# A new order for the mixer of a macaron layer, interleaved score products, and a second norm whose squares are summed by a matrix of ones

## The chip, the cores and the metric

One core of one Trainium2 chip runs the whole layer as a single program. The metric is the device time of one execution in microseconds (us): the median of several runs. A change of this kernel by less than about 0.2% (1.6 us) can't be told from no change.

## The reference

One encoder layer on x of 512 tokens by 1024 channels, in float32: half a SwiGLU feed-forward, a mixer, another half feed-forward, and a last norm. The mixer is the part that the change touches:

```python
def rmsnorm(x, g):
    y = x * lax.rsqrt(jnp.mean(x * x, axis=-1, keepdims=True) + EPS)
    return y * g

def hybrid_mixer(h, w_in, q_gain, k_gain, rel_bias, pool_w, pool_scale, w_out):
    proj = h @ w_in                       # 1024 -> q, k, v, u of 512 columns each
    ...
    a = chunked_attention(q, k, v, q_gain, k_gain, rel_bias)   # 8 heads of 64, q and k normed per head
    p = multiscale_pool(u, pool_w, pool_scale)                 # 4 groups, windows 2, 4, 8, 16
    return jnp.concatenate([a, p], axis=-1) @ w_out

x = x + 0.5 * swiglu_ffn(rmsnorm(x, ffn1_norm), ...)
x = x + hybrid_mixer(rmsnorm(x, mix_norm), ...)
x = x + 0.5 * swiglu_ffn(rmsnorm(x, ffn2_norm), ...)
x = rmsnorm(x, final_norm)
```

Attention is causal by chunks of 64 frames (own chunk and 8 before), with a bias that depends on the distance alone.

## The kernel before, in words

**Products.** Everything is kept transposed, with channels on the partitions and the 512 tokens along the free axis, in eight tiles x[0] to x[7]. A float32 product is made as three products of rounded parts (`mm3`, L270 to L276): high by high (L274), low by high (L275), high by low (L276). A split into high and low parts is a cast or scale on ACT (L157, L160) and a subtraction on DVE (L158, L161), and weights of the mixer are split by L1235 on ACT and L1237 on DVE. `mm3` streams its moving operand "woven" (L252): column 0, column 256, column 1, column 257 and so on, and whoever reads the result takes it apart again with `back` (L255), a strided read of PSUM.

**Stages.** The first feed-forward runs to about 321 us of the trace, the mixer to about 475 us, the second feed-forward and the last norm to the end. There are eight PSUM banks, four for `mm` tiles and four for `a` tiles.

**The mixer** is a set of coroutines that the program runs while it is built: `products` (the projections in the order of `ORDER`: q and k of heads 0 to 3, q and k of heads 4 to 7, u, v, u, u, u, then the output projection), `finish_norm`, `qk_norm`, `scores` for each pair of heads, `softmax` for each head and tile of 128 queries, `head` (transposes of the probabilities, L1506, and the product with v, L1518), `pool` and `pool_map`. Each yields when it would have to wait, by a model of four clocks (`on`, `until`), and the first one in order of rank that can run goes on (`run_parts`, L1160). The result is a fixed order of instructions for each of PE, ACT, DVE and GpSimd. So the numbers `RANK_...`, `RANKS`, `SLACK`, `POOL_AFTER`, `NORM`, `NORM_AT` and `FILL_AT` at the head of the file set the order and nothing else; the hardware then waits on semaphores.

**The second norm.** The squares of x are added up into `acc`, a 128x512 tile (L385). `per_token` (L387) multiplies `acc` by a column of ones, four 128x1 products in full float32 (L389), which gives the sum of squares of each token on its partition. ACT takes a rough inverse root of it (L396) and DVE makes one Newton step (L360 to L362); the result is `r`, 128x4, by which q, k and v are scaled when they leave PSUM (L1315, L160/L161). For u, where tokens lie along the free axis, the same numbers are needed along rows: DVE writes two diagonal matrices with the high and low parts of `r` (L401 to L405), PE multiplies them by ones (L414), and ACT copies the bank to `rb` (L422), which L1567 uses.

**q and k.** The four token tiles of a q and k projection leave their banks by L1315 on ACT (times `r`), are squared by L1331 on ACT, summed per head by L1334 on DVE, go through the integer-started root L337 to L349 on DVE, are scaled by L1365 on DVE, and are transposed by L1374 on PE.

**Scores.** For a pair of heads, the two lie in rows 0 to 63 and 64 to 127 of the same tiles, so L1454 issues two products at a time, one in each half of the array, into two banks. `GROUPS` lists for each pair which query tiles share a bank: pair 0 has ((2, 0),) and then ((3,), (1,)), pairs 1 and 3 have (1, 0), (2,), (3,), and pair 2 the reverse. `softmax`: bias and row maximum on DVE (L1416), exponent on ACT (L1423), reciprocal on DVE (L1426), scaling on ACT (L1429).

**v and u.** Each 128x512 tile of v leaves its bank in two halves, each by L160 on ACT and then L161 on DVE. u leaves by L1567 on DVE, and GpSimd makes the trailing sums (L1577).

## Time and profile before

| what | value |
|---|---|
| runs | 807.75, 807.83, 808.76 us; median 807.83 |
| the profiled execution's own time | 808.83 us |
| its span, first to last instruction | 807.0 us (1.83 us lie outside it) |
| mean granted TensorE clock | 0.999 |
| DVE, ACT, GpSimd busy | 88%, 62%, 12% of the span |
| instructions | 14153 |

In a line of the timeline the first two numbers are start and duration in us, then come the engine, the line of the kernel, the operation, the output and the input, and how many such instructions in a row were taken together; in brackets stands how long the engine was idle before it, and on whom it waited. PE's matmuls overlap: a 128x512 product is shown with 0.38 us, but one starts every 0.216 us, so PE's time is read from one start to the next.

### The profile page before, as it was taken

What the parts mean: (1) busy time and instruction counts of PE and PEld (TensorE: products, weight loads), DVE (VectorE), ACT (ScalarE), POOL (GpSimd) and SP (SyncE); (2) the same over time, 40 slices, a digit from 0 to 9 for tenths busy, and PEclk for the clock granted to TensorE, in tenths of its full rate; (3) what the DMA queues carried; (4) which work ended last, traced back from release to release, by engine and by line L of the source; (5) the groups of instructions that cost most, each with busy time, mean ns of one, the idle gap of its engine ahead of it and who ended that gap; (6) DMA issues with size and microseconds to landing.
All of it is one profiled execution on the core that took longest, in us unless ns stands there. A gap on an engine that the chain in (4) does not pass through costs nothing.

```text
span 807.0 us, 14153 instructions
## 1 busy us (share of the span) xinstructions
PE 797.8 (99%) x5273; PEld 735.5 (91%) x5273; DVE 710.3 (88%) x1163; ACT 503.8 (62%) x873; POOL 100.1 (12%) x148
## 2 busy tenths in 40 slices
PE   9999999999999999999999999999999999999996
PEld 8889999999988888888878888899999999988886
DVE  7999999899897878876979778999989999896997
ACT  8456555666676657558657756565566655766574
POOL 0111111222011100101111000201121111010100
PEclk9999999999999999999999999999999999999999
DMA  8677778988799973332212137858878888799942
GB/s 311 184 210 203 185 214 247 208 201 216 200 270 314 310 241 105 118 118 92 78 54 79 53 132 250 268 160 224 216 213 230 213 199 210 222 305 339 320 144 104
DMA packets 79414, 160.61 MB, mean 199 GB/s; under 512 B 7393, under 2 KB 30705, under 8 KB 78961
## 3 DMA queue, kind: packets, MB, share of 16 engines
q1 hardware_dynamic: 56256, 113.16, 41.7%
q0 software_dynamic: 22656, 46.14, 27.2%
q8 instruction: 41, 0.67, 0.3%
q10 hardware_dynamic: 432, 0.41, 0.1%
q14 instruction: 29, 0.23, 0.1%
HBM read 153.38 MB, written 50.34 MB: 252 GB/s over the span
## 4 chain that ended last, share of the span: by engine, by line
PE 86%; DVE 7%; ACT 4%; issue 2%; DMA 1%; SPq 0%; DVEq 0%; ACTq 0%
PE mm L274 20%; PE mm L275 20%; PE mm L276 20%; PE a L276 7%; PE a L275 7%; PE a L274 7%; DVE wlo L158 1%; PE a L1518 1%; PE a L1506 1%; ACT prob L1423 1%; ACT prob L1429 1%; ACT whi L1235 1%; PE a L1454 1%; DVE prob L1416 1%; DVE wlo L1237 1%
## 5 line engine op out<-in xcount | busy, mean ns | idle before, releaser
L158 DVE TENSOR_TENSOR wlo<-raw,whi 128x1024 fp32r<-128x1024 f32 (+1 forms) x110 | 120.6, 1107 | 17.7 <-ACT whi L157 17.6
L157 ACT CAST whi<-raw 128x1024 fp32r<-128x1024 f32 (+1 forms) x110 | 103.2, 951 | 38.1 <-PE mm L276 14.8
L939 POOL DMA_DIRECT2D wsum<-in_wB_dram x72 | 70.2, 1086 | 447.8 <-DVE t L843 222.1
L275 PE MATMUL mm<-ha,whi 128*128 128x256 f32 x420 | 115.5, 275 | 0.0
L276 PE MATMUL mm<-ha,wlo 128*128 128x256 f32 x420 | 115.5, 275 | 0.0
L274 PE MATMUL mm<-ha,whi 128*128 128x256 f32 x420 | 115.5, 275 | 0.0
L788 ACT ACTIVATE t<-mm 128x256 f32<-128x256 f32 x105 | 40.4, 385 | 113.6 <-PE mm L276 113.1
L600 DVE TENSOR_TENSOR wlo<-wsum,whi 128x1024 fp32r<-128x1024 f32 x70 | 85.5, 1221 | 9.8 <-ACT whi L595 9.8
L274 PEld LDWEIGHTS mm<-ha,whi 128*128 128x128 f32 x420 | 80.6, 192 | 0.1
L275 PEld LDWEIGHTS mm<-ha,whi 128*128 128x128 f32 x420 | 80.6, 192 | 0.1
L276 PEld LDWEIGHTS mm<-ha,wlo 128*128 128x128 f32 x420 | 80.6, 192 | 0.0
L595 ACT CAST whi<-wsum 128x1024 fp32r<-128x1024 f32 x70 | 70.0, 1047 | 3.7 <-DVE wsum L619 2.0
L275 PE MATMUL mm<-wlo,ah 128*128 128x512 f32 x176 | 67.0, 380 | 0.1
L276 PE MATMUL mm<-whi,ah 128*128 128x512 f32 x176 | 66.7, 379 | 0.0
L274 PE MATMUL mm<-whi,ah 128*128 128x512 f32 x176 | 66.5, 379 | 0.0
L274 PE MATMUL mm<-hhi,whi 128*128 128x512 f32 x168 | 64.5, 384 | 0.0
L600 DVE TENSOR_TENSOR wlo<-raw,whi 128x512 fp32r<-128x512 f32 x70 | 64.1, 955 | 0.0
L275 PE MATMUL mm<-hlo,whi 128*128 128x512 f32 x168 | 63.7, 379 | 0.0
L276 PE MATMUL mm<-hhi,wlo 128*128 128x512 f32 x168 | 63.7, 379 | 0.0
L595 ACT CAST whi<-raw 128x512 fp32r<-128x512 f32 x70 | 57.9, 828 | 1.9 <-PE mm L275 1.9
L158 DVE TENSOR_TENSOR ah<-acts,ah 128x512 fp32r<-128x512 f32 (+1 forms) x72 | 45.7, 646 | 10.9 <-ACT ah L157 10.8
L157 ACT CAST ah<-acts 128x512 fp32r<-128x512 f32 (+1 forms) x72 | 40.6, 581 | 20.4 <-PE mm L275 13.8
(246 smaller groups left out, 2331.6 us busy)
## 6 DMA issues: line engine op xcount, KB each, us to landing
raw<-in_wA_dram SPq DMA_DIRECT2D x142, 256.0 KB, 3.9
wsum<-in_wB_dram POOLq DMA_DIRECT2D x60, 512.0 KB, 7.2
raw<-wsum SPq DMA_DIRECT2D x40, 512.0 KB, 6.3
raw<-in_wB_dram SPq DMA_DIRECT2D x30, 512.0 KB, 8.4
wsum<-wsum POOLq DMA_DIRECT2D x20, 512.0 KB, 5.7
raw<-in_wA_dram SPq DMA_DIRECT2D x16, 512.0 KB, 4.6
x<-in_xT_dram SPq DMA_DIRECT2D x16, 256.0 KB, 6.4
raw<-in_wQK_dram SPq DMA_DIRECT2D x8, 512.0 KB, 3.4
```

Source lines behind the costliest of these rows:

```text
L157: last_cast[0] = nc.scalar.copy(hi, src)
L158: nc.vector.tensor_tensor(lo, src, hi.bitcast(F32), op=ALU.subtract)
L274: nc.tensor.matmul(acc, a[0], b[0], start=start, stop=False, **more)
L275: nc.tensor.matmul(acc, a[0], b[1], start=False, stop=False, **more)
L276: return nc.tensor.matmul(acc, a[1], b[0], start=False, stop=stop, **more)
L595: nc.scalar.copy(hi, src)
L600: nc.vector.tensor_tensor(lo, src, hi.bitcast(F32), op=ALU.subtract)
L788: nc.scalar.activation(two(dst), back(src), AF.Copy, scale=scale)
L939: begun = nc.gpsimd.dma_start(self.rows(i, g), self.rows(self.terms[i][at], g), **(dict(accum_op=ALU.add) if at else {}),)
L1235: nc.scalar.copy(hi, raws[i])
L1237: nc.vector.tensor_tensor(lo, raws[i], hi.bitcast(F32), op=ALU.subtract)
L1416: nc.vector.tensor_tensor_reduce(p, sc, bias[h][0][:, S - n :], -1.0, BIG, op0=ALU.add, op1=ALU.min, accum_out=nm)
```

## The change

**The second norm.** `finish_norm` no longer calls `per_token` and `spread`. It splits `acc` into high and low parts (ACT, DVE) and sends them through two 128x512 products with a matrix of ones (`over_rows`, the call that the third norm uses in `steps`, L425). Every row of the bank then holds the sum of squares of all 512 tokens. From it DVE picks each token's own sum with the identity (four 128x128 multiply-and-add reductions), ACT and DVE make `r` as before, and ACT (one 128x512 root) and DVE (128x512 `v`, then three more 128x512 operations in the new part `spread`) make `rb` without PE.

**The scores.** The moving operand is now woven, so softmax reads the bank through `back`. With `SHARED = 1, 2`, the second head of pairs 1 and 2 is to take the upper half of the first head's bank wherever a group is `(1,)` alone.

**The order.** The ranks and the numbers for the clocks are replaced, `NORM_AT` goes from 3 to 2, `FILL_AT` from 7 to 6, `AHEAD_AT` from 8 to 7.

```diff
-RANK_QK, RANK_HEAD, RANK_POOL, RANK_SCORES = 1.66, 1.47, 0.935, 0.92
+RANK_QK, RANK_HEAD, RANK_POOL, RANK_SCORES = 1.82, 1.42, 1.335, 0.82
-POOL_AFTER = (8, 8, 7, 6)
+POOL_AFTER = (7, 3, 5, 7)
+SHARED = 1, 2
-            nc.vector.tensor_tensor_reduce(
-                p, sc, bias[h][0][:, S - n :], -1.0, BIG, op0=ALU.add, op1=ALU.min, accum_out=nm
+            nc.vector.tensor_tensor_reduce(
+                two(p), back(sc), two(bias[h][0][:, S - n :]), -1.0, BIG, op0=ALU.add, op1=ALU.min,
+                accum_out=nm,
             )
...
-                for _ in group:
+                for ts in group:
                     sc.append([])
-                    for h in heads:
-                        sc[-1].append((yield from take("a")))
+                    for i in range(2):
+                        if i and ts == (1,) and pair in SHARED:
+                            sc[-1].append((sc[-1][0][0][:, S // 2 :], sc[-1][0][1]))
+                        else:
+                            acc = yield from take("a")
+                            sc[-1].append((acc, ["a"] * len(ts) * (2 if ts == (1,) and pair in SHARED else 1)))
...
-                                    kT[pair][0][b][rows, :n], start=a + b == 0, stop=a == 1,
+                                    woven(kT[pair][0][b][rows, :n]), start=a + b == 0, stop=a == 1,
...
         def finish_norm():
             while used[0] < NORM_AT:
                 yield None
+            pair = temp(F32R), temp(F32R)
+            split(n2.acc, *pair)
+            f = on("dve", t_dve(S), on("act", t_act(S)))
+            yield from until(f + NORM)
             total = yield from take("a")
-            n2.per_token(total)
-            f = on("dve", NORM, on("pe", 0.45))
+            n2.over_rows(total, pair)
+            f = on("pe", 0.45)
+            yield from until(f, "act", "dve")
+            total = back(total)
+            wide, junk = temp(), temp()
...
+            for t in range(NT):
+                z = slice(t % 2 * P, (t % 2 + 1) * P)
+                nc.vector.tensor_tensor_reduce(
+                    junk[:, :P], total[:, t // 2, z], ident, 1.0, 0.0, op0=ALU.mult, op1=ALU.add,
+                    accum_out=ss[:, t : t + 1],
+                )
+                f = on("dve", t_dve(P))
+            nc.scalar.activation(root, ss, AF.Abs_reciprocal_sqrt, scale=1.0 / D, bias=eps)
+            nc.vector.tensor_scalar(v, ss, 1.0 / D, EPS, op0=ALU.mult, op1=ALU.add)
+            rsqrt_of(v, root, n2.r)
+            on("dve", 0.8, on("act", 0.3))
+            nc.scalar.activation(
+                two(wide), total, AF.Abs_reciprocal_sqrt, scale=1.0 / D, bias=eps
+            )
+            nc.vector.tensor_scalar(two(junk), total, 1.0 / D, EPS, op0=ALU.mult, op1=ALU.add)
+            f = on("dve", t_dve(S), on("act", t_act(S)))
             room["a"].append(f)
-            yield from until(f)
-            wide = yield from take("a")
-            n2.spread(wide)
-            room["a"].append(on("act", t_act(S), on("pe", 0.9)))
+            start(spread(wide, junk, f), 8)
+
+        def spread(y, v, f):
+            yield from until(f, "dve")
+            sq = temp()
+            nc.vector.tensor_tensor(sq, y, y, op=ALU.mult)
+            nc.vector.scalar_tensor_tensor(v, sq, -0.5, v, op0=ALU.mult, op1=ALU.mult)
+            n2.rb = n2.broadcast()
+            nc.vector.scalar_tensor_tensor(n2.rb, v, 1.5, y, op0=ALU.add, op1=ALU.mult)
+            on("dve", 3 * t_dve(S))
```

How the instructions stand, at three places. The numbers behind the names tell tiles apart; the line numbers after the change are 22 to 28 higher (L274 is L296, L414 is L436, L161 is L183, L1429 is L1453).

PE in the q and k projection of heads 4 to 7, before: the four 128x1 products of the norm stand between the products of the sixth weight tile with token tiles 0 and 1 (`mm_4128` and `mm_4132` are the banks of those token tiles).

```order
L275 MATMUL mm_4128<-wlo_4122,hhi_4040 128x512
L276 MATMUL mm_4128<-whi_4121,hlo_4041 128x512
L389 MATMUL a_4215<-ones,acc_3897 128x1 x4
L274 MATMUL mm_4132<-whi_4121,hhi_4040 128x512
L275 MATMUL mm_4132<-wlo_4122,hhi_4040 128x512
```

and seven products of `mm3` further on, still before, the pair with ones that makes `rb`:

```order
L274 MATMUL mm_4140<-whi_4121,hhi_4053 128x512
L275 MATMUL mm_4140<-wlo_4122,hhi_4053 128x512
L276 MATMUL mm_4140<-whi_4121,hlo_4054 128x512
L414 MATMUL a_4259<-t_4234,ones_r 128x512
L414 MATMUL a_4259<-t_4235,ones_r 128x512
L274 MATMUL mm_4128<-whi_4176,hhi_4066 128x512
L275 MATMUL mm_4128<-wlo_4177,hhi_4066 128x512
```

The same stretch of PE's row after, where the pair with ones makes the sums themselves:

```order
L296 MATMUL mm_4128<-whi_4121,hhi_4053 128x512
L297 MATMUL mm_4128<-wlo_4122,hhi_4053 128x512
L298 MATMUL mm_4128<-whi_4121,hlo_4054 128x512
L436 MATMUL a_4231<-t_4185,ones_r 128x512
L436 MATMUL a_4231<-t_4186,ones_r 128x512
L296 MATMUL mm_4132<-whi_4121,hhi_4053 128x512
L297 MATMUL mm_4132<-wlo_4122,hhi_4053 128x512
L298 MATMUL mm_4132<-whi_4121,hlo_4054 128x512
```

L389 has no counterpart, and the pair with ones stands three `mm3` (nine products) earlier among its neighbours; the number of products with ones is the same.

DVE while v leaves its banks (`mm_4728`, `mm_4732`, `mm_4742`, `mm_4775` before are the banks of the four tiles of v; `bias` is the widened bias of a head, `m` a half of a pooled group or of a transposed q or k, `wlo` a weight's low part), before:

```order
L1237 TENSOR_TENSOR wlo_4980<-raw_4852,whi_4979 128x1024
L161 SCALAR_TENSOR_TENSOR v_4996<-mm_4728,r_4222,v_4996 128x4x64 x2
L1426 RECIPROCAL rt_4963<-tot_4962 128x1
L1274 STREAM_SHUFFLE bias_5006<-t_4770 128x256
L161 SCALAR_TENSOR_TENSOR m_5014<-a_5001,ps_sb,m_5013 128x512
L161 SCALAR_TENSOR_TENSOR v_5020<-mm_4732,r_4222,v_5020 128x4x64 x2
L1274 STREAM_SHUFFLE bias_5025<-t_4770 128x256
L161 SCALAR_TENSOR_TENSOR v_5036<-mm_4742,r_4222,v_5036 128x4x64 x2
L1237 TENSOR_TENSOR wlo_5045<-raw_4891,whi_5044 128x1024
L161 SCALAR_TENSOR_TENSOR v_5054<-mm_4775,r_4222,v_5054 128x4x64 x2
```

and after, from the same weight split on:

```order
L1259 TENSOR_TENSOR wlo_4991<-raw_4865,whi_4990 128x1024
L180 TENSOR_TENSOR m_5003<-t_4960,m_5002 128x512
L183 SCALAR_TENSOR_TENSOR v_5009<-mm_4731,r_4242,v_5009 128x4x64 x2
L183 SCALAR_TENSOR_TENSOR v_5020<-mm_4736,r_4242,v_5020 128x4x64 x2
L183 SCALAR_TENSOR_TENSOR v_5032<-mm_4747,r_4242,v_5032 128x4x64 x2
L183 SCALAR_TENSOR_TENSOR m_5041<-a_5028,ps_sb,m_5040 128x512
L1259 TENSOR_TENSOR wlo_5048<-raw_4903,whi_5047 128x1024
L183 SCALAR_TENSOR_TENSOR v_5057<-mm_4795,r_4242,v_5057 128x4x64 x2
```

Two shuffles, and the 128x1 reciprocal of a 128x512 softmax, no longer stand between the halves of v; they are issued earlier. The `ps_sb` operation has moved behind the third tile, and the subtraction of a pooled group (L158, now L180) stands right before the first half.

DVE ahead of the normalising of the probabilities of heads 4 and 5 on ACT (`rt` is the reciprocal of a softmax row sum, `us` and `u` a pooled group's sums and input, `m` again a half of a pooled group), before:

```order
L1584 SCALAR_TENSOR_TENSOR t_5249<-us_5222,u_5168 128x512
L1589 TENSOR_TENSOR edge_5251<-us_5222,inv_count 128x7
L1590 TENSOR_TENSOR t_5249<-edge_5251,u_5168 128x7
L1567 TENSOR_TENSOR u_5267<-mm_5160,rb_4262 128x512
L158 TENSOR_TENSOR m_5288<-t_5249,m_5287 128x512
L1426 RECIPROCAL rt_5212<-tot_5211 128x1
L1426 RECIPROCAL rt_5227<-tot_5226 128x1
L1416 ISA prob_5302,nm_5303<-a_5244,bias_4645 128x256
L1416 ISA nm_5303 128x1
```

and after:

```order
L1612 SCALAR_TENSOR_TENSOR t_5265<-us_5246,u_5175 128x512
L1617 TENSOR_TENSOR edge_5267<-us_5246,inv_count 128x7
L1618 TENSOR_TENSOR t_5265<-edge_5267,u_5175 128x7
L1595 TENSOR_TENSOR u_5270<-mm_5163,rb_4277 128x512
L1450 RECIPROCAL rt_5215<-tot_5214 128x1
L1450 RECIPROCAL rt_5228<-tot_5227 128x1
L1438 ISA prob_5289,nm_5290<-a_5245,bias_4649 128x256
L1438 ISA nm_5290 128x1
L1438 ISA prob_5294,nm_5295<-a_5245,bias_4649 128x128
L1438 ISA nm_5295 128x1
L180 TENSOR_TENSOR m_5303<-t_5265,m_5302 128x512
```

The pooled group's subtraction (L158, now L180) stood between u and the two reciprocals; now the reciprocals, and a 128x256 and a 128x128 softmax, come ahead of it.

## The prediction on record

> **What bounds the kernel now.** First the busy shares and the chain that ended last, from the profile's page:
>
> ```profile
> PE 797.8 (99%) x5273; PEld 735.5 (91%) x5273; DVE 710.3 (88%) x1163; ACT 503.8 (62%) x873; POOL 100.1 (12%) x148
> PE 86%; DVE 7%; ACT 4%; issue 2%; DMA 1%; SPq 0%; DVEq 0%; ACTq 0%
> ```
>
> PE is busy for 99% of the span, so the time can fall only where PE has less to do or where one of its few waits goes. The waits of PE:
>
> ```profile
> PE a L1518 <- DVE v L161: 1.3, 1, 1.3
> ```
>
> That is the only one of any size inside the mixer, and it lies in a stretch that the change reorders. The timeline then shows three places where products don't follow each other at their pace; they are quoted where they are used. So I add up, place by place, what PE gets back, in the profiled execution's clock (808.83 us, 1.0 above the median of 807.83), and take the sum off the median.
>
> **Term A: the second norm.** PE around the norm, and at the tightest bank behind it:
>
> ```profile
> 333.80 0.95 PE L389 MATMUL a<-ones,acc 128*128 128x1 f32 x8
> 334.61 0.46 PE L274 MATMUL mm<-whi,hhi 128*128 128x512 f32 x1
> 334.91 0.38 PE L275 MATMUL mm<-wlo,hhi 128*128 128x512 f32 x1
> ...
> 339.23 0.63 PE L414 MATMUL a<-t,ones_r 128*128 128x512 f32 x2
> 339.70 0.38 PE L274 MATMUL mm<-whi,hhi 128*128 128x512 f32 x1
> ...
> 346.82 0.42 PE L274 MATMUL mm<-whi,hhi 128*128 128x512 f32 x1
> 347.08 0.38 PE L275 MATMUL mm<-wlo,hhi 128*128 128x512 f32 x1
> ```
>
> From 334.91 to 339.23 stand 20 products, 0.216 each: that is PE's pace, for operands read woven. The four float32 columns take from 333.80 to 334.61, 0.81, and the product after them 0.30 instead of 0.216: 0.89 in all. They go. The pair with ones (339.70 - 339.23 = 0.47) stays a pair, only with another operand, so it costs what it did.
>
> Whether PE keeps the 0.89 depends on who frees its banks. The second q and k projection needs its fourth bank back from ACT:
>
> ```profile
> 339.90 0.58 ACT L422 COPY rb<-a 128x512 f32<-128x512 f32 x1 [4.85 <-PE a L414]
> 340.38 1.05 ACT L1235 CAST whi<-raw 128x1024 fp32r<-128x1024 f32 x1
> 341.34 0.68 ACT L1315 ACTIVATE t<-mm,r 128x512 f32<-128x512 f32 x1
> ...
> 346.03 0.68 ACT L1315 ACTIVATE t<-mm,r 128x512 f32<-128x512 f32 x1
> ```
>
> The fourth L1315 ends at 346.71, and the product at 346.82 is followed only after 0.26: there is no slack, and ACT's row from 339.90 on has no gap. So ACT must become 0.85 earlier as well. What it and DVE do instead is seen in the third norm, which already works in the new way, and in the reductions of softmax (a timeline of ACT and of DVE, then two groups by shape and place):
>
> ```profile
> 491.94 0.69 ACT L432 ACTIVATE t<-a,table 128x512 f32<-128x512 f32 x1 [1.78 <-PE a L414]
> ```
>
> ```profile
> 492.66 0.69 DVE L436 TENSOR_SCALAR t<-a 128x512 f32<-128x512 f32 x1 [1.35 <-ACT t L432]
> ...
> 494.71 0.69 DVE L443 SCALAR_TENSOR_TENSOR rb<-t,t 128x512 f32<-128x512 f32 x1
> ```
>
> ```profile
> L1416 DVE CUSTOM_DVE_ANT_0 prob<-a,bias 128x128 f32<-128x128 f32 x6 | 1.7, 286 | 0.0
> ```
>
> ```profile
> 334.55 2.63 DVE L1237 TENSOR_TENSOR wlo<-raw,whi 128x1024 fp32r<-128x1024 f32 x2
> ...
> 337.56 0.16 DVE L362 SCALAR_TENSOR_TENSOR r<-rs,root 128x4 f32<-128x4 f32 x1
> ```
>
> Before, `r` is there at 337.72. After: DVE ends its two weight splits at 337.18 and the low part of `acc` (about 0.65, as the other 128x512 operations) stands between them, so 337.8; the sums leave PE at about 337.1 (the pair starts twelve products after 333.80, at 336.4) and are not waited for. Four 128x128 reductions at 0.21 to 0.29 each make 0.85 to 1.15, the four small operations 0.6, so `r` comes at 339.3 to 339.6. It is wanted by the first L1315, whose bank PE fills by 339.70 + 6 x 0.216 - 0.89 = 340.1: cover 0.5 to 0.8. ACT loses the 0.58 copy that held it until 339.90 and gets the wide root of 0.69 at about 339.0; its weight cast then starts at 339.3 to 339.7 instead of 340.38, and the first L1315 at 340.3 to 340.6 instead of 341.34, 0.75 to 1.0 earlier. DVE's three wide operations for `rb` end near 343.6; they hold scratch tiles that the third square on ACT (L1331) takes, due at that moment. I take **-0.85**. Bounds: -0.94 (all of it, and the 0.05 at 347.08), and +0.4 if one weight split of 1.22 comes between DVE and those tiles.
>
> **Term B: the wait for v.** PE at the first product with v, then DVE:
>
> ```profile
> 406.26 0.92 PE L1518 MATMUL a<-pT,v 128*128 128x512 f32 x4
> 408.47 0.71 PE L1518 MATMUL a<-pT,v 128*128 128x128 f32 x4 [1.29 <-DVE v L161]
> ```
>
> ```profile
> 400.36 0.48 DVE L161 SCALAR_TENSOR_TENSOR v<-mm,r,v 128x256 fp32r<-128x256 f32 x1
> ...
> 401.85 0.44 DVE L1274 STREAM_SHUFFLE bias<-t 128x256 f32<-128x256 f32 x1
> 402.19 0.74 DVE L161 SCALAR_TENSOR_TENSOR m<-a,ps_sb,m 128x512 fp32r<-128x512 f32 x1
> ...
> 405.86 0.48 DVE L161 SCALAR_TENSOR_TENSOR v<-mm,r,v 128x256 fp32r<-128x256 f32 x1 [0.54 <-ACT v L160]
> 406.79 1.22 DVE L1237 TENSOR_TENSOR wlo<-raw,whi 128x1024 fp32r<-128x1024 f32 x1 [0.45 <-ACT whi L1235]
> 407.93 0.48 DVE L161 SCALAR_TENSOR_TENSOR v<-mm,r,v 128x256 fp32r<-128x256 f32 x1
> ```
>
> The last tile's first half ends at 408.41 and the product goes on at 408.47. Six halves take 5.50 (400.36 to 405.86) because the pooled operation and the shuffles stand among them, then comes the weight split. After, the halves stand together: 1.0 from a tile's first half to its second, 0.4 to 0.5 on to the next tile, about 3.9 in all. They start later, at 400.9, since the root chain of q and k ahead of them gets later (the second rival), so the sixth is at 404.8. The pooled operation now follows (0.66 from start to start), then ACT's cast and DVE's split, which ends about 407.4, and the last tile's half is done at 407.9: the wait ends 0.5 earlier. **-0.5**; bounds 0 (the start is late by another 0.5) and -1.3 (the wait gone).
>
> **Term C: a wait for the softmax of heads 4 and 5.** DVE, ACT and PE there:
>
> ```profile
> 425.33 1.46 DVE L158 TENSOR_TENSOR m<-t,m 128x512 fp32r<-128x512 f32 x1 [0.29 <-ACT m L157]
> ```
>
> ```profile
> 426.96 1.23 ACT L1429 ACTIVATE prob<-prob,rt 128x512 f32<-128x512 f32 x2 [0.92 <-DVE rt L1426]
> ```
>
> ```profile
> 433.86 0.38 PE L276 MATMUL mm<-m,wlo 128*128 128x512 f32 x1
> 434.38 0.86 PEld L1506 LDWEIGHTS a<-ident,prob 128*128 128x128 f32 x8 [0.55 <-ACT prob L1429]
> ```
>
> PE loses 0.52 - 0.22 = 0.3 at 434.38, because ACT, without a gap from 426.96 on, scales the 128x256 probabilities too late; and it was idle for 0.92 before, since the reciprocal stood behind the pooled subtraction of 1.46. Now the reciprocal stands ahead of it, ACT is about 0.8 earlier, and the transposes find their input: **-0.3**, bounds 0 and -0.3.
>
> **Term D: the scores and the rest.** A block of 128x512 scores of pair 0:
>
> ```profile
> 379.97 0.96 PE L1454 MATMUL a<-m,m 64*128 64x512 f32 x6
> 380.86 0.48 PE L274 MATMUL mm<-whi,hhi 128*128 128x512 f32 x1
> ```
>
> Three pairs take 0.89, of which three times 0.216 is 0.65; the rest is mostly the change to half rows and back, which stays. At most 0.08 per block of weaving is to be had, and less at the narrower widths: over 4 pairs and 4 widths 0 to 0.3 altogether. The bank sharing does nothing: `(1,)` alone is a group of pair 0 only, and `SHARED` names pairs 1 and 2, so the score products stand as before. DVE reads the strided bank at its pace, as L436 does above (0.69, like the operations that read SBUF). The transposes of head 1 move earlier, between products, with a margin near zero against ACT: 0 to +0.2. One weight cast of the second feed-forward moves a step later and is needed 6 us after. GpSimd's and SP's queues keep their order but for one bias load. I take **-0.1**, bounds -0.3 and +0.2.
>
> On the woven read a page speaks against the change: the Trainium skill, "SBUF — State Buffer", section "Door 1: The DMA port swizzle", says that SBUF is read in lines of 16 bytes and that accesses which each go to another line pay. A woven operand alternates between two places 256 elements apart. By the 20 woven products above, at 0.216 each, the trace shows no such price at full rows; only with half rows is it unseen.
>
> **The sum.** -0.85 - 0.5 - 0.3 - 0.1 = -1.75: 807.1 for the profiled execution, 806.1 for the median. Beyond the mixer PE carries the shift along, since its later inputs come from engines that follow it.
>
> **Rivals.**
>
> *The norm's new chain is late.* Half a microsecond on ACT or DVE between 337 and 344 is felt in full at the fourth bank: A is then -0.35 and the time 806.6. For it: ACT has no gap there; against: it loses as much as it gets. Chance 0.10.
>
> *DVE is shut out by GpSimd, and the transposes of q and k wait (slower).* GpSimd's adds, DVE's blocked operation, its last step, and PE's first transpose:
>
> ```profile
> 381.81 3.58 POOL L1577 TENSOR_TENSOR us<-us 128x525 f32<-128x525 f32 x3
> ```
>
> ```profile
> 384.17 1.26 DVE L1341 TENSOR_SCALAR var<-ms 128x16 f32<-128x16 f32 x1
> ...
> 389.02 2.49 DVE L1365 TENSOR_TENSOR t<-t,z 128x512 f32<-128x512 f32 x4
> ```
>
> ```profile
> 392.20 0.60 PE L1374 MATMUL a<-ident,t 128*128 128x128 f32 x4
> ```
>
> A tiny L1341 took 1.26 and ended at 385.43, just after the adds (385.39). Now u leaves PSUM about 1.0 later and the adds with it, while a 128x512 softmax and reciprocals come ahead of L1340. I have the chain 1.0 later: L1365 done at 392.5, against 392.85 for the transposes (three products later). From 0.3 more, PE waits. If two more adds of 1.2 are sat out, that is +2.1 at the transposes, and B falls to -0.2: -0.85 + 2.1 - 0.2 - 0.3 - 0.1 = +0.65, 808.5; with a third, 809.7. Against: before, only one operation was held for one add. Chance 0.07, half of it over 809.4.
>
> *A DMA-bound stage eats the gain.* ACT's waits between 715 and 760 us:
>
> ```profile
> ACT whi L157 <- DMA raw<-wsum: 4.7, 4, 2.0
> ```
>
> If these loads don't move up with PE, up to 1.3 is given back: 807.4. Against: they are issued when PE and DVE free their buffers, and PE itself hardly waits there. Chance 0.12.
>
> *Woven half rows are slow (slower).* If every stream of L1454 took twice its pace, 12 pairs at each width would add 12 x (0.216 + 0.162 + 0.108 + 0.054) = 6.5: 812.6. It decides from a quarter of that on. Chance 0.03, as the page's rule is not borne out by the 0.216 above.
>
> *More than I count:* v's wait all gone and weaving at its best: 805.1 or less. Chance 0.08.
>
> **How the numbers follow.** My forecast has 0.56, the rest 0.04 (nothing gained at all, or effects that cancel). 0.2% of 807.83 is 1.6 us, about what can be told from no change, so faster starts below 806.2, in the middle of my forecast's own range of 805.3 to 806.9: of its 0.56 I count 0.40 as faster. With 0.08 above that is 0.48; slower is 0.03, 0.04 and 0.02 of the rest, 0.09; the same 0.43. The range runs from 804.9 (B and D at their best) to 808.0, which leaves out the slow cases and the farthest of the gains.
>
> **What would show it.** Right: no 128x1 products near 334 and the fourth bank's product at about 345.9; the wait for v at about 0.8; L1506 after the output projection's first products without a gap; 128x512 scores with a woven operand at 0.22 a pair. Wrong: a gap of PE before the products that reuse the fourth bank, at the first L1374, or a longer wait of PE for v; L1454 blocks longer than 0.89; PE waiting for weights after 715.

## The result, and the profile after

| | runs | median, us | lowest to highest, us |
|---|---|---|---|
| before | 11 | 808.41 | 807.72 to 809.46 |
| after | 11 | 806.01 | 805.83 to 806.79 |

The ratio is 0.9972, its 95% interval 0.9965 to 0.998: the changed kernel is faster, by 1.6 to 2.8 us. The profiled execution of it took 806.01 us, with a span of 804.2 and a granted clock of 0.999. One later execution, of the norm alone (914.86 us), ran at a granted clock of 0.851 and is counted in that kernel's median below, not in its ratio. The page's busy shares and its chain, after:

```profile
span 804.2 us, 14158 instructions
...
PE 795.8 (99%) x5265; PEld 734.1 (91%) x5265; DVE 712.7 (89%) x1172; ACT 504.5 (63%) x874; POOL 100.1 (12%) x148
...
PE 90%; DVE 5%; ACT 2%; issue 1%; DMA 1%; SPq 0%; DVEq 0%
```

PE is busy for 2.0 us less (797.8 before) and has 8 instructions fewer; in the chain its share rose from 86% to 90%, and DVE's fell from 7% to 5%. Its waits:

```profile
PE a L1546 <- DVE v L183: 0.4, 1, 0.4
```

The wait for v is down from 1.3 to 0.4. A wait of 0.2 for a reciprocal is new; its row stands below, at 379.79.

**How much of it is the mixer.** The two profiled executions are 2.8 us apart, but not all of that is the change. I read the mixer from the start of one product behind the first feed-forward to the start of the first row of eight transposes behind the output projection (whose last product starts at 485.64 before, not at 475); the code between them is what the change touches. Before, then after, from PE's timelines:

```profile
324.22 0.46 PE L275 MATMUL mm<-wlo,hhi 128*128 128x512 f32 x1
...
494.27 0.80 PE L1748 MATMUL a<-ident_r,xr 128*128 128x128 f32 x8
```

```profile
323.71 0.46 PE L297 MATMUL mm<-wlo,hhi 128*128 128x512 f32 x1
...
491.75 0.81 PE L1808 MATMUL a<-ident_r,xr 128*128 128x128 f32 x8
```

The stretch took 494.27 - 324.22 = 170.05 and takes 491.75 - 323.71 = 168.04: 2.0 less. The other 0.8 lies outside: the same first feed-forward ended 0.5 later in the execution of before, and what follows the stretch took 312.7 there and 312.5 here (807.0 - 494.27 and 804.2 - 491.75). Over all the profiles of this study the stretch begins anywhere from 323.2 to 324.2 with the same instructions ahead of it, and what follows it takes 312.5 to 313.6. So single times are compared below only through the stretch.

**Where the 2.0 went.** Summing PE's time from each start to the next over the stretch, by what it computes:

| PE's work, with the waits ahead of it | before | after | difference |
|---|---|---|---|
| products with ones, for the norms | 1.92 | 1.28 | -0.65 |
| products with v | 11.45 | 10.53 | -0.92 |
| output projection | | | -0.30 |
| scores and transposes of probabilities | 16.96 | 17.02 | +0.06 |
| u and the pooled map | | | -0.21 |
| q, k and v | | | +0.03 |

They add up to -1.99. The rows behind the first two, from PE's timeline of after:

```profile
335.88 0.80 PE L436 MATMUL a<-t,ones_r 128*128 128x512 f32 x2
336.51 0.38 PE L296 MATMUL mm<-whi,hhi 128*128 128x512 f32 x1
...
345.36 0.38 PE L298 MATMUL mm<-whi,hlo 128*128 128x512 f32 x1
345.63 0.48 PE L296 MATMUL mm<-whi,hhi 128*128 128x512 f32 x1
345.95 0.38 PE L297 MATMUL mm<-wlo,hhi 128*128 128x512 f32 x1
...
405.39 0.92 PE L1546 MATMUL a<-pT,v 128*128 128x512 f32 x4
406.75 0.71 PE L1546 MATMUL a<-pT,v 128*128 128x128 f32 x4 [0.45 <-DVE v L183]
```

The 128x1 columns are gone. The pair with ones takes 336.51 - 335.88 = 0.63, where the pair of before took 0.47. At the fourth bank the product at 345.63 comes 0.27 after the one ahead of it and is followed after 0.32, where before it came at the pace of 0.216 and was followed after 0.26. With v, the two groups are 1.36 apart, where they were 2.21.

### The profile page after: what moved, and what is told of

Read it like the earlier page. It is cut to its first block, busy times and chain, and to the rows that moved or that the text cites. A ratio compares the mean times of both kernels' runs of the same rounds, so it can differ in the third digit from the quotient of the medians.

```text
span 804.2 us, 14158 instructions
## 1 busy us (share of the span) xinstructions
PE 795.8 (99%) x5265; PEld 734.1 (91%) x5265; DVE 712.7 (89%) x1172; ACT 504.5 (63%) x874; POOL 100.1 (12%) x148
## 4 chain that ended last, share of the span: by engine, by line
PE 90%; DVE 5%; ACT 2%; issue 1%; DMA 1%; SPq 0%; DVEq 0%
PE mm L296 21%; PE mm L297 21%; PE mm L298 21%; PE a L298 8%; PE a L296 7%; PE a L297 7%; PE a L1546 1%; PE a L1534 1%; PE a L1482 1%; DVE wlo L180 1%; DMA raw<-in_wA_dram 1%; ACT whi L179 1%; ACT hhi L182 0%; DVE ah L180 0%; DVE prob L1438 0%
## 5 line engine op out<-in xcount | busy, mean ns | idle before, releaser
L180 DVE TENSOR_TENSOR wlo<-raw,whi 128x1024 fp32r<-128x1024 f32 (+1 forms) x110 | 120.0, 1101 | 16.0 <-ACT whi L179 16.0
L296 PE MATMUL mm<-ha,whi 128*128 128x256 f32 x420 | 115.5, 275 | 0.0
L296 PEld LDWEIGHTS mm<-ha,whi 128*128 128x128 f32 x420 | 80.6, 192 | 0.1
L296 PE MATMUL mm<-whi,ah 128*128 128x512 f32 x176 | 66.6, 379 | 0.0
L296 PE MATMUL mm<-hhi,whi 128*128 128x512 f32 x168 | 64.5, 384 | 0.0
L180 DVE TENSOR_TENSOR ah<-acts,ah 128x512 fp32r<-128x512 f32 (+1 forms) x72 | 45.3, 639 | 11.8 <-ACT ah L179 11.6
```

Source lines behind the costliest of these rows:

```text
L180: nc.vector.tensor_tensor(lo, src, hi.bitcast(F32), op=ALU.subtract)
L296: nc.tensor.matmul(acc, a[0], b[0], start=start, stop=False, **more)
```

## The experiments

The theory that I went in with is the prediction's own: the norm, the order and the weaving each give their part, and GpSimd's adds hold DVE once. The times of the kernels; each ratio is against before on the same chip, where the median of before was 808.41 to 808.54:

| kernel | median (runs), us | ratio to before, 95% interval | stretch, us |
|---|---|---|---|
| before | 808.41 (11) | | 170.05 |
| after | 806.01 (11) | 0.9972, 0.9965 to 0.998 | 168.04 |
| norm alone | 807.93 (11) | 0.9993, 0.9984 to 1.0002 | 169.48 |
| weaving alone | 808.12 (11) | 0.9994, 0.9986 to 1.0003 | 169.81 |
| order alone | 807.56 (11) | 0.9985, 0.9976 to 0.9994 | 169.01 |
| bank not shared | 806.15 (6) | 0.9971, 0.9958 to 0.9983 | 168.12 |
| head 1 later | 806.15 (1) | | 168.60 |
| two sums left out | 806.50 (1) | | 167.92 |
| first sum on DVE | 806.12 (1) | | 168.39 |
| products with ones later | 805.73 (1) | | 168.13 |
| wide root first | 806.14 (1) | | 168.24 |
| split behind v | 805.06 (1), 805.20 (5) | 0.9963, 0.9949 to 0.9976 | 167.34, 167.34 |
| wide root first, split behind v | 805.75 (5) | 0.9964, 0.9951 to 0.9978 | 167.51 |

### The three parts, one by one

**The norm alone**: the kernel before with the new `finish_norm`.

```diff
-ACT_FIX, DVE_FIX, QK_NORM, NORM = 0.09, 0.1, 3.7538, 3.08
+ACT_FIX, DVE_FIX, QK_NORM, NORM = 0.09, 0.1, 3.7538, 5.8
-AHEAD, NORM_AT, FILL_AT, QK_ROOT = 2, 3, 7, ()
+AHEAD, NORM_AT, FILL_AT, QK_ROOT = 2, 2, 7, ()
...
-            n2.per_token(total)
+            n2.over_rows(total, pair)
...
-            n2.spread(wide)
+            start(spread(wide, junk, f), 8)
...
```

> The kernel before with the new second norm alone (finish_norm, spread, NORM 5.8, NORM_AT 2); order, scores and everything else as before. Theory 1, the parts add up and everything behind follows PE: PE is earlier by about 0.6 us from the norm on (0.89 for the float32 columns, less about 0.25 given back at the pair with ones and at the fourth bank, as the profile after shows), the wait for v stays near 1.45 us from start to start (406.85 to 408.47 before), and the mixer is 0.6 shorter. Theory 2, DVE's chain sets the time at v whatever PE gains ahead of it: the 0.6 come back there, the spacing at v grows from 1.62 to about 2.2, and the mixer is as long as before within 0.1.

The stretch is 0.56 shorter. The place of v on PE:

```profile
404.88 0.92 PE L1518 MATMUL a<-pT,v 128*128 128x512 f32 x4
407.11 0.71 PE L1518 MATMUL a<-pT,v 128*128 128x128 f32 x4 [1.31 <-DVE v L161]
```

The wait for v is what it was (407.11 - 404.88 = 2.23): the norm has no part in that term. The median is 0.5 lower, an amount that the runs alone can't tell from nothing.

**The weaving alone**: the kernel before, with the score products' moving operand woven.

```diff
-                p, sc, bias[h][0][:, S - n :], -1.0, BIG, op0=ALU.add, op1=ALU.min, accum_out=nm
+                two(p), back(sc), two(bias[h][0][:, S - n :]), -1.0, BIG, op0=ALU.add, op1=ALU.min, accum_out=nm
...
-                                    kT[pair][0][b][rows, :n], start=a + b == 0, stop=a == 1,
+                                    woven(kT[pair][0][b][rows, :n]), start=a + b == 0, stop=a == 1,
```

> The kernel before with woven operands in the score products and the strided read in softmax, and nothing else. Theory 1: all score blocks together are shorter by 0.4 us (a 128x512 block about 0.84 instead of 0.89), and the mixer by the same. Theory 2: the share of pairs 0 and 1, about 0.2, comes back in the wait for v, and the mixer is shorter by 0.2. The prediction's term for it was 0 to 0.3 with 0.1 taken. If the woven read of half rows cost anything, blocks would be longer than 0.89.

A block of 128x512 scores of pair 0 in it:

```profile
378.87 0.92 PE L1454 MATMUL a<-m,m 64*128 64x512 f32 x6
379.71 0.48 PE L274 MATMUL mm<-whi,hhi 128*128 128x512 f32 x1
```

It takes 0.84, where it took 0.89. Over the stretch PE's score products take 0.40 less, and PE gives 0.16 of it back in small waits elsewhere: the stretch is 0.24 shorter. So woven half rows are a gain here, and the rival by which they would be slow is gone. Why the woven read is the shorter one, no run shows.

**The order alone**: the changed kernel with the old norm and with plain scores.

```diff
-ACT_FIX, DVE_FIX, QK_NORM, NORM = 0.09, 0.1, 3.7538, 5.8
+ACT_FIX, DVE_FIX, QK_NORM, NORM = 0.09, 0.1, 3.7538, 3.08
-AHEAD, NORM_AT, FILL_AT, QK_ROOT = 2, 2, 6, ()
+AHEAD, NORM_AT, FILL_AT, QK_ROOT = 2, 3, 6, ()
...
-                                    woven(kT[pair][0][b][rows, :n]), start=a + b == 0, stop=a == 1,
+                                    kT[pair][0][b][rows, :n], start=a + b == 0, stop=a == 1,
...
```

> The kernel after with the old second norm and with unwoven scores, so the new order alone. Theory 1: -0.95 us in the mixer: -0.85 at v, -0.3 at the transposes of head 4, -0.2 at a pooled group's product, and +0.45 where the transposes of head 1 are cut in two and wait for DVE and ACT. Theory 2: the same parts, but the +0.45 is not seen in the end, because a later PE waits less for v: then the gain at v is more than 0.85 here only if PE comes later, and norm and weaving that were absorbed in the two runs before leave about -2.0 for the order.

```profile
406.08 0.92 PE L1545 MATMUL a<-pT,v 128*128 128x512 f32 x4
407.38 0.71 PE L1545 MATMUL a<-pT,v 128*128 128x128 f32 x4 [0.39 <-DVE v L183]
```

The stretch is 1.04 shorter, and the wait for v is down to 0.39 without the new norm. By class: products with v -0.98, output projection -0.31, u and the pooled map -0.21, and scores and transposes +0.46. The last is a cost that only the order brings, and in the whole change the weaving pays for it.

Norm, weaving and order add up to -0.56 - 0.24 - 1.04 = -1.84, against -2.00 for the whole: nothing large hangs on their working together.

**The shared bank**, undone in the changed kernel.

```diff
-SHARED = 1, 2
+SHARED = ()
```

> The kernel after with SHARED empty. If the prediction's reading is right, that no group of pairs 1 and 2 is (1,) alone, this is the same program instruction for instruction, so the mixer has the same length within 0.02 us and the time is that of the kernel after; what differs shows how much one execution differs from the next outside the mixer. If sharing does take place, the products of pairs 1 and 2 stand otherwise, and a difference of more than 0.1 us shows in the score blocks.

Every engine gets the same instructions in the same order, and the time is the same (806.15 against 806.01, the stretch 168.12 against 168.04). The edit of `SHARED` does nothing, since `(1,)` alone is a group only in pair 0. As a second run of one program it also shows how finely the stretch can be read: to about 0.1.

### What the +0.46 is

After, the first transposes of head 1 stand between the scores and the products; PE's timeline of after:

```profile
378.71 0.92 PE L1482 MATMUL a<-m,m 64*128 64x512 f32 x6
379.79 0.63 PE L1534 MATMUL a<-ident,prob 128*128 128x128 f32 x4 [0.17 <-DVE rt L1450]
380.43 0.48 PE L296 MATMUL mm<-whi,hhi 128*128 128x512 f32 x1
```

The block takes 379.79 - 378.71 = 1.08, where the weaving alone has 0.84: the four transposes come 0.24 late. They then take 0.64, where eight together, the row at 432.05 that is shown further below, take 0.80 to the next row, 0.10 each, so four would take 0.40. That is 0.24 twice, 0.48 in all, and covers the +0.46. The next kernel lets them come later in the program.

```diff
+                if h == 1 and group == (1, 3):
+                    yield from until(clock["pe"] + 1.0)
```

> The kernel after with one delay: the first transposes of head 1 (L1534 behind the 128x512 scores of pair 0) are issued one mm3 later, and both groups of four in one piece; a pooled group's product and a few evacuations shift with them. In the kernel after this place costs PE 0.45 to 0.5 us (0.22 of waiting and the split into two groups). Theory 1, the costs add up: scores and transposes together take 0.45 less, the wait for v stays at 0.77 from start to start, the mixer is 167.6 instead of 168.04. Theory 2, the end of v's evacuation is set by DVE whatever PE does: PE comes to the product with v 0.45 earlier and waits 0.45 longer, 1.2 from start to start, and the mixer stays within 0.1 of 168.04.

PE at the same place:

```profile
378.34 0.92 PE L1482 MATMUL a<-m,m 64*128 64x512 f32 x6
380.05 0.48 PE L296 MATMUL mm<-whi,hhi 128*128 128x512 f32 x1 [0.80 <-DVE u L1597]
```

The stretch is 0.56 longer than after, so neither theory holds. From the block to the next product PE takes 380.05 - 378.34 = 1.71 without the transposes, and it took 380.43 - 378.71 = 1.72 with them. It waits 0.80 for DVE to take u out of the bank that the product needs, and the transposes had filled that wait. DVE at u, before and after:

```profile
379.83 0.69 DVE L1567 TENSOR_TENSOR u<-mm,rb 128x512 f32<-128x512 f32 x1
```

```profile
379.70 0.67 DVE L1595 TENSOR_TENSOR u<-mm,rb 128x512 f32<-128x512 f32 x1
```

Before, u was out at 380.52, which is 0.34 ahead of the product at 380.86. After, it is out at 380.37, and the product follows 0.06 later, at 380.43. Measured from the start of the block, u is out after 1.66 (380.37 - 378.71), where it was 0.55 (380.52 - 379.97). So the 0.48 isn't the price of the transposes: it is the rest of a wait for u, which the new order takes out of its bank later, and the transposes made it smaller.

### The wait for v: does GpSimd's lock set it?

The prediction had the root chain of q and k (from L1340, now L1362) held up behind GpSimd's adds, and v's evacuation after it. GpSimd and DVE, after:

```profile
381.67 3.56 POOL L1605 TENSOR_TENSOR us<-us 128x525 f32<-128x525 f32 x3
```

```profile
384.06 1.19 DVE L1362 TENSOR_SCALAR var<-ms 128x16 f32<-128x16 f32 x1
...
388.92 2.48 DVE L1387 TENSOR_TENSOR t<-t,z 128x512 f32<-128x512 f32 x4
...
399.72 0.47 DVE L183 SCALAR_TENSOR_TENSOR v<-mm,r,v 128x256 fp32r<-128x256 f32 x1
```

The small L1362 takes 1.19 and ends at 385.25, as the adds do (385.23). The next kernel leaves out two of the trailing sums of the fourth pooled group.

```diff
+                    if g == 3 and step >= 4:
+                        f = on("pool", 1.25) - HOP
+                        step = 2 * step
+                        continue
```

> The kernel after, with the last two of the four GpSimd sums of the first pooled group left out (its window is 4 instead of 16); every other engine's order is as before. If the 1.19 us of L1362 are GpSimd's doing, L1362 takes 0.17, the root chain and the four L1387 behind it end 1.0 earlier, the halves of v come 1.0 earlier, and PE waits for v no more (0.77 from start to start falls to 0.2): the mixer is 167.4 to 167.5. If L1362 waits for something else, nothing moves: 168.04.

```profile
384.07 0.18 DVE L1362 TENSOR_SCALAR var<-ms 128x16 f32<-128x16 f32 x1
...
388.08 2.48 DVE L1387 TENSOR_TENSOR t<-t,z 128x512 f32<-128x512 f32 x4
...
399.52 0.48 DVE L183 SCALAR_TENSOR_TENSOR v<-mm,r,v 128x256 fp32r<-128x256 f32 x1
```

Without the adds L1362 takes 0.18, so it was GpSimd that held it for a microsecond. The Trainium skill, "SBUF — State Buffer", section "Who interferes with whom", says that DVE and GpSimd share a pair of ports, that whoever issues first keeps it for its whole instruction, and that DVE's tensor_scalar is among those that can ask for it; the 1.19 against 0.18 agrees.

But that chain sets little of v's time. L1387 is 0.84 earlier, and the first half of v, 399.72 after, comes only 0.20 earlier (the wait for v is 0.26). Between them DVE now waits for ACT, which takes PE's transposes of q and k out of their bank, and PE starts these at 391.98 in both traces. The stretch is 0.12 shorter, about the finest that can be read. The same by another way, which computes everything: DVE makes the first of the four sums, so that GpSimd is done earlier.

```diff
+                if g == 3:
+                    s = mpool.tile([P, PAD + S + 40], F32, tag="us", name=name("us"), bufs=2)
+                    nc.vector.tensor_tensor(
+                        s[:, 1 : PAD + S], u[:, 1 : PAD + S], u[:, : PAD + S - 1], op=ALU.add
+                    )
+                    step = 2
...
+                    if g == 3 and step == 2:
+                        f = on("pool", 1.25) - HOP
+                        yield from until(f, "pool")
```

> The kernel after, with the first of the four sums of the first pooled group on DVE, right behind u, instead of GpSimd; the other three stay, every other order is as it was. DVE has 0.6 us more work ahead of the root chain, GpSimd ends about 0.5 earlier (three sums of 1.19 from 381.1 instead of four from 380.5). If the two engines shut each other out for a whole instruction, L1362 then starts at 384.6, after the last sum or 0.1 before its end, takes 0.2 to 0.3, and the chain ends 0.4 to 0.5 earlier: the wait for v falls from 0.77 to about 0.35 and the mixer is 167.6. If they don't, DVE is 0.6 later and the wait for v grows to 1.3: 168.6.

DVE, then PE's waits:

```profile
384.60 0.18 DVE L1362 TENSOR_SCALAR var<-ms 128x16 f32<-128x16 f32 x1
```

```profile
PE a L1534 <- DVE nm L1438: 0.3, 1, 0.3
```

L1362 takes 0.18 again, since GpSimd's last sum ends at 384.55, and the wait for v is 0.26. But L1362 starts only at 384.60, and DVE's extra sum delays a row maximum that PE's transposes wait for: the stretch is 0.35 longer.

So what does end the wait for v? DVE behind the sixth half, after:

```profile
403.57 0.48 DVE L183 SCALAR_TENSOR_TENSOR v<-mm,r,v 128x256 fp32r<-128x256 f32 x1 [0.54 <-ACT v L182]
404.15 0.75 DVE L183 SCALAR_TENSOR_TENSOR m<-a,ps_sb,m 128x512 fp32r<-128x512 f32 x1
405.08 1.22 DVE L1259 TENSOR_TENSOR wlo<-raw,whi 128x1024 fp32r<-128x1024 f32 x1 [0.18 <-ACT whi L1257]
406.22 0.48 DVE L183 SCALAR_TENSOR_TENSOR v<-mm,r,v 128x256 fp32r<-128x256 f32 x1
```

A weight split of 1.22 and the 0.18 it waited for stand ahead of the half that PE wants. The next kernel issues that one split (cast and subtraction) behind the last half of v.

```diff
...
-            nc.scalar.copy(hi, raws[i])
-            t = on("act", 0.98)
-            nc.vector.tensor_tensor(lo, raws[i], hi.bitcast(F32), op=ALU.subtract)
-            t = on("dve", t_dve(1024), t)
+            if i != 15:
+                split(raws[i], hi, lo)
+            else:
+                held.append((raws[i], hi, lo))
+            t = on("dve", t_dve(1024), on("act", 0.98))
...
+                if t == NT - 1:
+                    split(*held.pop())
```

> The kernel after with one weight split (cast on ACT, 1.04, and subtraction on DVE, 1.22, the one between the third and the fourth tile of v) issued behind the fourth tile of v; its weights are wanted by PE 15 us later. If this split is what PE waits for at v, the seventh half of v ends 1.2 to 1.9 earlier, at 404.8 to 405.5, before PE comes at 405.98, and the spacing of 0.77 falls to 0.17 to 0.2: the mixer is 167.45. If the halves are set by their start, at 399.7 behind the transposes of q and k, the fourth tile still gains the split's time and the result is the same; only if ACT or DVE are late otherwise, by the bank of the tile itself, does the wait stay: 168.0.

DVE, then PE:

```profile
404.57 0.48 DVE L183 SCALAR_TENSOR_TENSOR v<-mm,r,v 128x256 fp32r<-128x256 f32 x1
```

```profile
405.14 1.36 PE L1549 MATMUL a<-pT,v 128*128 128x512 f32 x8
```

The half comes at 404.57 instead of 406.22, and the eight products run as one row with no wait. The stretch is 0.70 shorter than after, and all of it lies here: the products with v take 9.82 over the stretch, where they took 10.53. The 0.45 in the bracket is less than that, because it counts only the time in which PE is shown idle, behind the end of the product ahead; from start to start the fifth product had come 0.77 after the fourth.

### What holds term A back

After, the pair with ones takes 0.16 longer than before. DVE and ACT around it:

```profile
335.26 0.88 DVE L180 TENSOR_TENSOR t<-acc,t 128x512 fp32r<-128x512 f32 x1
...
337.20 0.28 DVE L1735 CUSTOM_DVE_ANT_0 t<-a,ident 128x128 f32<-128x128 f32 x1
```

```profile
338.52 0.30 ACT L1740 ACTIVATE root<-r_lo,table 128x4 f32<-128x4 f32 x1 [4.51 <-DVE r_lo L1735]
...
340.22 0.69 ACT L1337 ACTIVATE t<-mm,r 128x512 f32<-128x512 f32 x1
...
344.89 0.68 ACT L1337 ACTIVATE t<-mm,r 128x512 f32<-128x512 f32 x1
```

The low part of `acc` ends at 335.26 + 0.88 = 336.14, after the first product with ones has started (335.88), so the second one waits for it. ACT waits for the last of the four reductions (L1735), starts at 338.52 and has no gap from there to the fourth L1337. The next kernel issues the pair three products later.

```diff
-ACT_FIX, DVE_FIX, QK_NORM, NORM = 0.09, 0.1, 3.7538, 5.8
+ACT_FIX, DVE_FIX, QK_NORM, NORM = 0.09, 0.1, 3.7538, 6.4
```

> The kernel after with the pair of products with ones one mm3 (0.65 us) later on PE; nothing else moves. The pair takes 0.63 from 335.88 in the kernel after, since DVE writes the low part of the sums until 336.14. Later it finds both parts: 0.47 or less, 0.16 gained at the pair. The sums come 0.5 later, at about 337.2 to 337.3, when DVE is done with its weight split (337.2): r comes 0 to 0.1 later. If the fourth bank is unchanged (0.15 lost there), the mixer is 167.9; if r's lateness reaches the bank in full, 168.0 as now.

```profile
336.16 0.59 PE L436 MATMUL a<-t,ones_r 128*128 128x512 f32 x2
336.59 0.38 PE L296 MATMUL mm<-whi,hhi 128*128 128x512 f32 x1
...
344.79 0.38 PE L298 MATMUL mm<-whi,hlo 128*128 128x512 f32 x1
345.29 0.48 PE L296 MATMUL mm<-whi,hhi 128*128 128x512 f32 x1
```

The pair takes 0.43 now, 0.20 less. At the fourth bank the step is 0.50, where it was 0.27: 0.23 more, and the stretch is the same (168.13). What PE saves at the pair it waits for at the bank, because ACT's fourth L1337 starts when it did, 121.2 after the start of the stretch in both. So the chain over DVE and ACT sets the end, and PE's own time there is slack.

That chain has one wide root on ACT (0.67) between the small one and the weight cast. The next kernel keeps the later pair and issues the wide root first, while DVE would be at its reductions.

```diff
+            nc.scalar.activation(
+                two(wide), total, AF.Abs_reciprocal_sqrt, scale=1.0 / D, bias=eps
+            )
             for t in range(NT):
...
-            nc.scalar.activation(
-                two(wide), total, AF.Abs_reciprocal_sqrt, scale=1.0 / D, bias=eps
-            )
```

> The kernel of the pair with ones one mm3 later, and in it ACT takes the wide 128x512 root as soon as the sums stand in PSUM, ahead of the four reductions' small root, instead of behind it. ACT is idle from 334 to 338.5 in the kernel after, so the wide root costs nothing there, and the weight cast and the four L1337 behind it come 0.57 earlier. If ACT's chain sets when the fourth bank comes free (the later pair alone gained 0.2 at the pair and lost 0.23 there), the products wait no more at the fourth bank: the mixer is 167.7 to 167.8, 0.3 shorter than after, all of it at norm and q and k products. If r, which comes at 339.4 from DVE, sets it, nothing is gained: 168.1.

ACT, then DVE, then PE:

```profile
337.15 0.69 ACT L1733 ACTIVATE t<-a,table 128x512 f32<-128x512 f32 x1 [3.21 <-PE a L436]
```

```profile
337.87 0.29 DVE L1738 CUSTOM_DVE_ANT_0 t<-a,ident 128x128 f32<-128x128 f32 x1 [0.65 <-ACT t L1733]
```

```profile
345.74 0.48 PE L296 MATMUL mm<-whi,hhi 128*128 128x512 f32 x1 [0.27 <-ACT t L1337]
```

The reductions don't run beside the root: they read the same bank, and the program makes them wait until ACT has read it, 0.65. ACT's first L1337 is 0.2 later (116.7 after the start of the stretch, where it was 116.5), and PE waits at the fourth bank again. The stretch is 0.2 longer than after. The Trainium skill, "PSUM — Partial Sum Buffer", section "PSUM bank collisions raise a hardware error", says that two engines reading one bank in the same partitions at once collide, so such reads have to be kept apart; no run here has the collision, only the wait that keeps them apart.

### The best version

Both edits together, and the split behind v alone with more runs:

> The kernel after with the three edits of the two runs before: pair with ones one mm3 later, wide root first, weight split behind v. If the gains add up: 167.15 in the mixer, 0.9 below the kernel after, 805.1 for the median. If a later wait takes part of it (the head products behind v wait for DVE's delayed split of the head's output), 167.5 and 805.5.

> The kernel after with the one weight split issued behind the fourth tile of v, now timed. Its mixer was 167.34 in one profile, 0.70 shorter than the kernel after. If that holds, the median is 805.2 to 805.4 and the ratio to the kernel before 0.9961 to 0.9965; if a later stage takes it back, 806.0 as the kernel after.

With both, the median is 805.75 and the stretch 167.51; the split behind v alone has 805.20 and 167.34, so the first edit adds nothing; PE again gains 0.20 at the pair with ones and loses 0.37 by the fourth bank. In the second profile of the split behind v PE again goes through its eight products with v without a wait. The version is faster than before (interval 0.9949 to 0.9976) and by its medians 0.8 faster than after; the two intervals overlap, so that last step rests on the traces, where the stretch was 0.70 shorter in both profiles.

## Why the prediction was right or wrong, point by point

- **The sum** (-1.75): the mixer lost 2.0 in the profiles, and the medians are 2.4 apart. The 806.1 was close to the 806.01 partly because the median of the first three runs of before, 807.83, stood 0.6 under that of eleven. It was also luck inside the sum: A came out 0.2 smaller than forecast and B 0.35 larger. The low end of the range, 804.9, doesn't come out of its own terms: B and D at their best take 0.8 and 0.2 off 806.1, which is 805.1.
- **A** (-0.85): the mechanism was right and the size was off: -0.56 alone, and -0.62 in the whole. Gone are the 0.81 of the columns and 0.08 of the product behind them, as said. The step that failed is "the first L1315 at 340.3 to 340.6 instead of 341.34, 0.75 to 1.0 earlier". Counted from the start of the stretch, the first L1315 came at 117.12, and as L1337 it comes at 116.51: 0.61 earlier, and the fourth 0.63. The term that was mis-sized ahead of it is the four reductions, put at 0.85 to 1.15: from the first to ACT's start they take 338.52 - 337.20 = 1.32. PE shows the missing part at two places. The pair with ones, of which the prediction said that "it costs what it did", takes 0.16 more, because `acc`'s low part took 0.88 and not 0.65, and the fourth bank costs 0.11 more (0.27 and 0.32 against the pace and 0.26). The later pair moved the one loss into the other, so ACT's chain is what holds PE: it is the rival of the late chain that took the missing part. I had it at -0.35 in all, and the truth lies between.
- **B** (-0.5): -0.85 (2.21 to 1.36). The halves stand together as foretold: six in 403.57 - 399.72 = 3.85, against 3.9. The step that failed is "They start later, at 400.9, since the root chain of q and k ahead of them gets later", by 1.0. The chain's last operation, L1387, ended at 388.92 + 2.48 = 391.40, where it had ended at 391.51; beside PE's transposes (391.98, before 392.20) it got 0.1 later. And little of such a delay reaches v: with two sums left out, 0.84 on the chain was worth 0.20 there. The halves started at 399.72, and PE at the products with v was itself 406.26 - 405.39 = 0.87 earlier: in the clock of before that is 400.59, 0.3 ahead of my number. The last tile's half ended at 406.70, in that clock 407.57 against my 407.9.
- **C** (-0.3): right. DVE and PE after:

```profile
423.17 0.21 DVE L1450 RECIPROCAL rt<-tot 128x1 f32<-128x1 f32 x2
423.84 1.17 DVE L180 TENSOR_TENSOR m<-t,m 128x512 fp32r<-128x512 f32 x1
```

```profile
431.84 0.38 PE L298 MATMUL mm<-m,wlo 128*128 128x512 f32 x1
432.05 1.04 PE L1534 MATMUL a<-ident,prob 128*128 128x128 f32 x8
```

  The reciprocals come ahead of the subtraction, and the transposes start 0.21 after the product, where it was 0.52. The order alone has the same gain (-0.31 at the output projection), so the order brings it; which of its moves does was not tried alone.
- **D** (-0.1): near in sum and wrong in its parts, so the sum was luck. The weaving gave 0.40 at the products (0.24 in the end), with a bound of 0.3. At the transposes of head 1 the order costs about 0.48, outside my bound of +0.2: I looked at their margin against ACT, and not at the bank of u behind them, which comes free later and would have cost more without them. And 0.2 came from u and the pooled map, which I had not counted: before, two steps of PE at 427.26 took 0.35 and 0.29 instead of 0.216, and after they follow at the pace. The shared bank did nothing, as said.
- **The rival of GpSimd's lock**: DVE was held once, 1.19, as before, and no more adds were sat out; PE's first transposes of q and k found their input:

```profile
391.98 0.60 PE L1396 MATMUL a<-ident,t 128*128 128x128 f32 x4
```

- **The rival of the DMA-bound stage**: it didn't show; what follows the stretch took 312.7 before and 312.5 after, and the medians are at least as far apart as the stretches.
- **The rival of the slow half rows**: the block of 0.84 speaks against it. The Trainium skill, "SBUF — State Buffer", section "Door 1: The DMA port swizzle", whose rule is that accesses which each go to another line of 16 bytes pay, is not borne out for this read by PE, neither at full rows (0.216) nor at half rows.
- **The signs that were named**: the wait for v fell further than to 0.8, to 0.45, and the fourth bank's product came 345.63 - 323.71 = 121.92 after the start of the stretch, where 345.9 would have been 121.68. Two of the signs of being wrong did show, too small to turn the result: PE's gap at the fourth bank (0.16 above the pace, where it was 0.04), and a block of L1482 that took 1.08 until the transposes behind it, which waited for a reciprocal.

## What to carry to other kernels

Where one engine is busy for 99%, count what a change gives at each place where its instructions don't follow at their pace, and then ask at each who frees what comes next: products that were saved on PE were lost again at the bank that ACT frees. An operation before the one that is waited for (here one weight split of 1.22 ahead of half a tile) is worth more than a whole chain made shorter upstream, if another engine's work lies in between. And measure a change of 2 us over the stretch that it touches, since the rest of the program differs by about as much from one execution to the next (1.0 ahead of the stretch and 1.1 behind it).

## What the runs showed of the hardware that I had not expected

- Interleaving the moving operand of products in half of the rows saved 0.05 of the 0.89 of a 128x512 block, and 0.40 over all score products.
- A 128x16 tensor_scalar on DVE was held for 1.0 us by one GpSimd add (1.19 against 0.18), while the 128x512 reductions just ahead of it ran beside the same adds in 0.68.
- The start of the mixer differed by 1.0 us (323.2 to 324.2) between executions with the same instructions ahead of it.
